# The first three token tiles in one layout, scales in the first transfer, ten products of ones, and two sums moved to GpSimd

## The chip, the cores and the metric

The kernel runs on one core of a Trainium2 chip. The metric is the device time of one execution in microseconds; the kernel is timed in several runs, and the median counts. One further execution is taken with the hardware profiler on. Engine names in profiles: PE is TensorE (matrix products), PEld its weight loads, DVE is VectorE, ACT is ScalarE, POOL is GpSimd, SP is SyncE, which issues most DMA transfers.

## The reference

One encoder layer is applied to two sequences, of 256 and of 2048 tokens, with 1024 features each, in float32:

```python
def encoder_layer(x, w_in, rpb, w_fourier, b_fourier, g_pre, g_na, g_f, w_out, g_post):
    h = rms_norm(x, g_pre)
    proj = h @ w_in
    q, k, v, z_a, u_f, z_f = jnp.split(proj, [...], axis=-1)   # six parts of 512 columns
    y_a = neighbourhood_attention(q, k, v, rpb)     # 8 heads of 64, window of 8 x 16 on a grid 64 wide
    y_f = fourier_mix(u_f, w_fourier, b_fourier)    # real part of a 2-D FFT, then a 512 x 512 product
    mixed = jnp.concatenate([rms_norm(y_a, g_na) * jax.nn.silu(z_a),
                             rms_norm(y_f, g_f) * jax.nn.silu(z_f)], axis=-1)
    out = mixed @ w_out
    return x + rms_norm(out, g_post)
```

## The kernel before

Every float32 product is made of three products: each operand is split into a high half (a cast, by ScalarE) and a low half (what is left over, by VectorE), and `mm3` (lines 159 to 162) adds high x high, high x low and low x high in PSUM. So nearly every operand costs one ScalarE pass and one VectorE pass over an SBUF tile before TensorE can use it. High halves have names ending in `h`, low halves in `l` (`wh`, `wl`; `xh`, `xl`; `vh`, `vl`).

The order of the instructions of every engine around the change is written by hand: each engine runs its own queue in program order and waits on semaphores. Stages in the order of the program, as far as the change touches them:

1. *Products of ones.* `onesq`, a 128 x 128 tile of ones, is set on GpSimd, and TensorE multiplies it with itself 13 times (line 225) while the first data travel.
2. *The start* (lines 611 to 639). The first three token tiles (two of the short sequence, `xt`; one of the long one, `xs`) hold 128 tokens each, with the 1024 features on the partitions in eight chunks of 128. They are loaded in four parts `kp` of two chunks each, one transfer of 128 KB per tile and part (`x_part`): the first part on ScalarE's queue, the others on SyncE's. The weights `wv` come on SyncE's queue, as does `gpre`, the eight chunks of norm scales. `split_w` makes the weights' halves, multiplied by the scales; `x_split` makes those of the tokens. The first useful product needs the first chunk of weights, the scales and the first token tile.
3. *Projections of three more tiles* (line 714 on). When `c == 4`, `xp` is made from the two tiles of the short sequence, the scales, and the tokens' norm factors, which come back from DRAM as a row broadcast over the partitions (`iv_get`, into a tile of the pool tag `vw`).
4. *Sixteen blocks for the short sequence* (lines 756 to 793). Block `b` multiplies one 128-column piece of `w_in` with the 256 tokens: 8 chunks x 3 products of 256 columns, 24 in all. `b_raw(b + 2)` splits the weights for two blocks later (ScalarE line 562 or 565, VectorE line 563 or 566). In between, VectorE prepares operands for the next stage, which forms its products from sums and differences of token quarters `nq` (512 token columns by four chunks, 128 x 2048 per tile): `n_scale` multiplies them by scale and norm factor (blocks 2 to 7), `n_sum` makes four sums (blocks 8 to 11, line 423), `n_first` splits the results (blocks 5, 12, 13; line 428 on ScalarE, line 429 on VectorE). Blocks 14 and 15 split the first weights of the next stage (`op_split`, lines 477 and 478).

The four sums depend on each other: the first writes a tile of its own, `t3`; the second overwrites `(0, 1)`, which the first reads; the third reads `t3` and overwrites `(0, 0)`, which the second reads; the fourth reads what the third wrote. Later in the kernel the same kind of work is done for the other half of the tokens, and there `b_split` (line 439) makes two of the low halves on GpSimd.

Of the kernel before, what the change touches and what calls it, by code (L numbers as in the profile page):

```python
# [10 lines left out]
F32 = mybir.dt.float32  # L11
F32R = mybir.dt.float32r
AF = mybir.ActivationFunctionType
ALU = mybir.AluOpType
# [3 lines left out]
TP, TS = 256, 2048  # L18
T = TP + TS
D = 1024  # L20
KC = 8
# [99 lines left out]
def layout(inp):  # L121
    a = {}
    x = np.concatenate([inp["x_prompt"].reshape(TP, D), inp["x_sample"].reshape(TS, D)], 0)
    a["xn"] = x
    a["xt"] = x[:TP].reshape(4, 2, 32, KC, 128).transpose(1, 4, 3, 0, 2).reshape(2, 128, KC, 128)
    a["xs"] = x[TP:TP + 1024].reshape(4, 4, 2, 32, KC, 128).transpose(0, 2, 5, 4, 1, 3).reshape(8, 128, KC, 128)
    a["xm"] = np.concatenate([x[:TP].reshape(4, 2, 32, D).transpose(1, 0, 2, 3).reshape(2, 128, D),
                              x[TP:].reshape(2, 16, 2, 32, D).transpose(0, 2, 1, 3, 4).reshape(16, 128, D)])
    a["xq"] = x[TP:].reshape(2, 4, 4, 2, 32, 2, 4, 128).transpose(0, 5, 3, 7, 6, 1, 2, 4).reshape(2, 2, 2, 128, 4, 512)
    w = inp["w_in"][0].reshape(KC, 128, 6, 512)  # L130
    q, k, v, za, u, zf = [w[:, :, i] for i in range(6)]
    a["wv"] = v.reshape(2, 4, 128, 512).transpose(0, 2, 1, 3)
    a["wu"] = u.reshape(4, 2, 128, 512).transpose(0, 2, 1, 3)
    a["wz"] = np.stack([m[:, :, h * 128:(h + 1) * 128].transpose(1, 0, 2) for m in (zf, za, k, q) for h in range(4)])
    rpb = inp["rpb"][0]

    d = np.arange(40)[None, :] - np.arange(32)[:, None]
    cols = np.clip(np.stack([d, d - 8]) + 15, 0, 30)
    rows = np.arange(4)[None, :] - np.arange(4)[:, None] + 7
    a["tp"] = rpb[:, rows[:, None, None, :, None], cols[None, :, :, None, :]].reshape(4, 2, 4, 2, 32, 4, 40) \  # L140
        .transpose(0, 2, 4, 3, 1, 5, 6).reshape(4, 128, 640)
    d = np.arange(32)[None, :] - np.arange(16)[:, None]
    cols = np.clip(np.concatenate([d[:, :24], d - 8, d[:, :24] - 8], 1) + 15, 0, 30)
    rows = np.clip(np.arange(15)[None, :] - np.arange(8)[:, None] + 3, 0, 14)
    a["tr"] = rpb[:, rows[:, None, :, None], cols[None, :, None, :]].reshape(8, 128, 1200)
    a["wf"] = inp["w_fourier"][0].reshape(4, 128, 512).transpose(1, 0, 2)
    a["bf"] = inp["b_fourier"][0].reshape(4, 128).T
    a["gpre"] = inp["g_pre"][0].reshape(KC, 128).T
    a["gmix"] = np.concatenate([inp["g_na"][0], inp["g_f"][0]]).reshape(8, 128).T
    a["wo"] = inp["w_out"][0].reshape(2, 4, 128, D)  # L150
    a["gpost"] = inp["g_post"][0].reshape(1, D)
    return {k: np.ascontiguousarray(v) for k, v in a.items()}
# [12 lines left out]
def build(tc, A, O):  # L165
    nc = tc.nc
# [28 lines left out]
    gpre = cst.tile([128, KC], F32, name="gpre")  # L195
# [12 lines left out]
    hp = ph.enter_context(tc.tile_pool(name="hp", bufs=1))  # L208
    st = ph.enter_context(tc.tile_pool(name="st", bufs=2))
# [11 lines left out]
    nc.gpsimd.memset(onesq, 1.0)  # L221

    idle = ps.tile([128, 512], F32, tag="c", name="idle", bufs=1)
    for x in range(13):
        nc.tensor.matmul(idle[:, :128], onesq, onesq, start=True, stop=True)

    def gt(shape, dtype, name):
        return gp.tile(shape, dtype, tag="g", name=name)

    def load(shape, src, name):  # L230
        t = gt(shape, F32, name)
        nc.sync.dma_start(t, src)
        return t

    US = [128, 2, 512]
    BS = [128, KC, 128]
    W = {"v": [], "u": []}
# [12 lines left out]
    def split_w(m, src, ks=range(2)):  # L250
        for k in ks:
            h, l = chunk(), chunk()
            g = gpre[:, len(W[m]):len(W[m]) + 1]
            nc.scalar.activation(h, src[:, k], AF.Copy, scale=g)
            nc.vector.scalar_tensor_tensor(out=l, in0=src[:, k], scalar=g, in1=h.bitcast(F32),
                                           op0=ALU.mult, op1=ALU.subtract)
            W[m].append((h, l))
# [9 lines left out]

    PL = [(None, b) for b in range(2)] + [(s, b) for s in range(NS) for b in range(2)]

    def xsrc(c):  # L270
        return A["xt"][c] if c < 2 else A["xs"][c - 2]

    def row_tile(c):
        s, b = PL[c]
        return c if s is None else 2 + 4 * b + s

    def xload(c):
        xs[c] = load(BS, xsrc(c), "xr")

    def x_split(c, ks=slice(0, 8)):  # L280
        if c not in xh:
            xh[c] = gt(BS, F32R, "xh"), gt(BS, F32R, "xl")
        h, l = xh[c][0][:, ks], xh[c][1][:, ks]
        nc.scalar.copy(h, xs[c][:, ks])
        nc.vector.tensor_tensor(out=l, in0=xs[c][:, ks], in1=h.bitcast(F32), op=ALU.subtract)


    def rows_load(i):
# [19 lines left out]
    ivb, ivr = {}, {}  # L308
# [8 lines left out]
        nc.sync.dma_start(ivD[c0:c0 + n], t)  # L317

    def iv_get(c0, n):
        t = ivb[c0] = hp.tile([128, 1024], F32, tag="vw", name="iv", bufs=3)  # L320
        nc.sync.dma_start(t[:, :128 * n],
                          ivD[c0:c0 + n].rearrange("(o c) p -> o (c p)", o=1).to_broadcast([128, 128 * n]))

# [57 lines left out]
    nq = {}  # L381
# [36 lines left out]
    def n_sum(x):  # L418
        if x == 0:
            nq["t3"] = k8(F32, "nt")  # L420
        o, i0, i1, op = (("t3", (1, 1), (0, 1), ALU.subtract), ((0, 1), (0, 1), (0, 0), ALU.subtract),
                         ((0, 0), "t3", (0, 0), ALU.add), ((1, 0), (0, 0), (1, 0), ALU.subtract))[x]
        nc.vector.tensor_tensor(out=nq[o], in0=nq[i0], in1=nq[i1], op=op)

    def n_first(j):
        src = nq[((0, 0), (1, 0), (0, 0), (0, 1), "t3", (1, 0), (1, 1))[j]]
# [177 lines left out]
    acc, xs, xh, xm = {}, {}, {}, {}  # L604
# [3 lines left out]
    part = lambda a, kp: a[:, kp % 2 * 2:kp % 2 * 2 + 2]  # L608


    def x_part(c, kp):
        if kp == 0:
            xs[c] = gt(BS, F32, "xr")
        ks = slice(2 * kp, 2 * kp + 2)
        (nc.sync if kp else nc.scalar).dma_start(xs[c][:, ks], xsrc(c)[:, ks])

    nc.sync.dma_start(RV[0][:, 0], A["wv"][0][:, 0])
    nc.sync.dma_start(gpre, A["gpre"])
    x_part(0, 0)
    x_part(1, 0)  # L620
    nc.sync.dma_start(RV[0][:, 1], A["wv"][0][:, 1])
    x_part(2, 0)
    nc.scalar.preload_act_table_set("natural_log_exp_and_others")
    nc.scalar.copy(warm, ones)
    for kp in range(4):
        ks = slice(2 * kp, 2 * kp + 2)
        v = part(RV[kp // 2], kp)
        if kp:
            nc.sync.dma_start(v, part(A["wv"][kp // 2], kp))
            for c in range(3):  # L630
                x_part(c, kp)
        split_w("v", v[:, 0:1], (0,))
        x_split(0, ks)
        if kp == 0:
            x_split(1, ks)
        split_w("v", v[:, 1:2], (0,))
        if kp:
            x_split(1, ks)
        x_split(2, ks)
# [74 lines left out]
    for c in range(3, 6):  # L714
        if c == 3:
            iv_get(0, 2)
        if c < 5:
            wz_load(3)
            x_split(c + 1)
        if c == 3:  # L720
            r_put(1)
        if c == 4:
            n_load((0, 0))
            iv_get(2, 8)
            r_put(2)
            xp = k8(F32, "xp", (128, KC, 256))
            hp_, lp_ = [k8(F32R, "p" + x, (128, KC, 256)) for x in "hl"]
            for k in range(KC):
                for t in range(2):
                    ts = slice(128 * t, 128 * t + 128)  # L730
                    nc.vector.scalar_tensor_tensor(out=xp[:, k, ts], in0=xs[t][:, k], scalar=gpre[:, k:k + 1],
                                                   in1=ivb[0][:, ts], op0=ALU.mult, op1=ALU.mult)
            nc.scalar.copy(hp_, xp)
            nc.vector.tensor_tensor(out=lp_, in0=xp, in1=f_(hp_), op=ALU.subtract)
        if c == 5:
            n_load((1, 0))
            b_raw(0)
            b_raw(1)
        p_mm("v", c, range(4))
        vu_out("v", c)  # L740
        if c == 5:
            b_raw(2)
            b_raw(3)
            wz_load(1)
            n_load((0, 1))
            n_scale(None, 0, 0)
            n_first(0)
        p_mm("u", c, range(4))
        if c == 3:
            iv_rows(2, 8)  # L750
        vu_out("u", c)
        if c == 3:
            iv_put(2, 8)


    for b in range(16):
# [13 lines left out]
        if 2 <= b < 8:  # L770
            x, y = divmod(b, 2)
            n_scale(None, *divmod(x, 2)[::-1], range(2 * y, 2 * y + 2))
        elif 8 <= b < 12:
            n_sum(b - 8)
        if b in (5, 12, 13):
            n_first((5, 12, 13).index(b) + 1)
        if b > 13:
# [1 line left out]
        p = mmt(512)[:, :TP]  # L779
# [3 lines left out]
        o = st.tile([128, 256], F32, tag="f", name="f", bufs=3)  # L783
# [51 lines left out]
    for i in range(16):  # L835
# [15 lines left out]
        o = [st.tile([128, 1024], F32, tag="f", name="f", bufs=3) for x in range(2)]  # L851
# [32 lines left out]
        for j in range(7):  # L884
            for f, d in ((u_load, 0), (u_split, 4), (u_stage1, 6)):
                x = 7 * pr + j - 7 - d
# [59 lines left out]
            p = mmt(512)  # L946
# [858 lines left out]
```

## Time and profile before

| | |
|---|---|
| median of 3 runs | 966.51 us (965.75 to 966.55) |
| the profiled execution, its own time | 965.94 us |
| its span, first to last instruction | 964.1 us |
| mean granted TensorE clock | 0.999 |
| TensorE busy | 955.2 us |
| VectorE busy | 703.4 us |
| ScalarE busy | 496.7 us |
| GpSimd busy | 427.0 us |

In the profile's rows, a time in front is the start in microseconds from the first instruction, then the duration; `L423` is a line of the kernel before; `out<-in` names tiles; `x4` is a count, and a row with a count shows the first start and the time that all of them cover. In square brackets stands how long the engine stood idle before the row, and what ended that.

### The profile page before, as it was taken

How to read it: one execution, taken by the hardware profiler on the slowest of the kernel's cores; microseconds unless marked ns; L12 is line 12 of the kernel's file. 1: busy time of each engine (PE TensorE's matmuls, PEld its weight loads, DVE VectorE, ACT ScalarE, POOL GpSimd, SP SyncE). 2: the span in 40 equal slices, each digit the busy share in tenths (PEclk: the TensorE clock that was granted, in tenths of full speed). 3: DMA queues.
4: the chain of work that ended last, by engine and by line, in shares of the span. 5: the costliest groups of instructions: out<-in, count | busy, mean ns of one | idle time of the engine just before them, and what ended most of it. 6: DMA issues, size and time to landing. Idle time of an engine off the chain costs nothing.

```text
span 964.1 us, 16993 instructions
## 1 busy us (share of the span) xinstructions
PE 955.2 (99%) x5743; PEld 799.0 (83%) x5743; DVE 703.4 (73%) x1310; ACT 496.7 (52%) x1077; POOL 427.0 (44%) x400
## 2 busy tenths in 40 slices
PE   9999999999999999999999999999999999999997
PEld 7889988888888888888888889888788887888886
DVE  5768978787876855687877458776765656659997
ACT  5845676423334532233344267677666676644443
POOL 2200002464751202674665043577677686524544
PEclk9999999999999999999999999999999999999999
DMA  8899796557848883499888896598877998979993
GB/s 304 317 354 380 248 348 243 199 203 263 298 185 345 299 347 123 181 362 360 308 294 327 306 335 225 169 285 292 258 235 238 287 285 286 301 253 346 332 353 122
DMA packets 140942, 269.81 MB, mean 280 GB/s; under 512 B 13402, under 2 KB 81840, under 8 KB 137464
## 3 DMA queue, kind: packets, MB, share of 16 engines
q1 hardware_dynamic: 140360, 268.32, 79.8%
q8 instruction: 46, 0.75, 0.3%
q10 hardware_dynamic: 432, 0.39, 0.2%
q14 instruction: 40, 0.33, 0.1%
q0 software_dynamic: 64, 0.02, 0.0%
HBM read 179.00 MB, written 96.81 MB: 286 GB/s over the span
## 4 chain that ended last, share of the span: by engine, by line
PE 96%; DVE 1%; DMA 1%; issue 0%; ACT 0%; DVEq 0%; SPq 0%; ACTq 0%
PE po L1454 20%; PE mm L161 18%; PE mm L160 18%; PE mm L162 18%; PE pv L1543 6%; PE ptb L1527 6%; PE s L1185 4%; PE pab L1022 2%; DMA wr<-wo 1%; PE py L160 1%; DMA gpre<-gpre 0%; PE py L162 0%; PE py L161 0%; PE ppq L1060 0%; PE pz L162 0%
## 5 line engine op out<-in xcount | busy, mean ns | idle before, releaser
L160 PE MATMUL mm<-xh,wa 128*128 128x512 f32 x448 | 174.4, 389 | 0.0
L162 PE MATMUL mm<-xh,wa 128*128 128x512 f32 x448 | 174.3, 389 | 0.0
L161 PE MATMUL mm<-xl,wa 128*128 128x512 f32 x448 | 174.3, 389 | 0.0
L532 POOL TENSOR_TENSOR ws<-wr 128x512 f32<-128x512 f32 x16 | 23.7, 1480 | 221.0 <-DVE vuo L505 123.8
L1219 POOL TENSOR_SCALAR w<-w,m 128x465 f32<-128x465 f32 (+9 forms) x136 | 84.7, 635 | 43.5 <-DVE m L1216 34.0
L162 PEld LDWEIGHTS mm<-xh,wa 128*128 128x128 f32 x448 | 84.1, 188 | 17.6
L160 PEld LDWEIGHTS mm<-xh,wa 128*128 128x128 f32 x448 | 84.1, 188 | 17.6
L161 PEld LDWEIGHTS mm<-xl,wa 128*128 128x128 f32 x448 | 84.1, 188 | 17.4
L1454 PE MATMUL po<-wo,yh 128*128 128x512 f32 x272 | 90.5, 414 | 0.0
L547 DVE TENSOR_TENSOR wa<-wr,wa 128x512 fp32r<-128x512 f32 x60 | 72.8, 1222 | 21.8 <-ACT wa L546 21.3
L1454 PE MATMUL po<-w,yh 128*128 128x512 f32 x280 | 86.8, 391 | 0.0
L1212 ACT ACTIVATE w<-w,m 128x465 f32<-128x465 f32 (+9 forms) x136 | 78.3, 579 | 13.3 <-DVE m L1207 12.9
L1207 DVE CUSTOM_DVE_ANT_1 w<-s,tb 128x465 f32<-128x465 f32 (+8 forms) x124 | 61.2, 531 | 9.8 <-PE s L1185 9.3
L161 PE MATMUL mm<-vl,xh 128*128 128x512 f32 x168 | 65.5, 390 | 0.2 <-DVE vl L478 0.2
L162 PE MATMUL mm<-vh,xl 128*128 128x512 f32 x168 | 65.4, 389 | 0.0
L160 PE MATMUL mm<-vh,xh 128*128 128x512 f32 x168 | 65.4, 389 | 0.0
L585 POOL TENSOR_TENSOR mt<-mt,rmask 128x880 f32<-128x880 f32 (+2 forms) x24 | 50.3, 2110 | 32.2 <-DVE mt L581 25.9
L1454 PEld LDWEIGHTS po<-w,yh 128*128 128x128 f32 x280 | 52.2, 188 | 10.9 <-issue 0.4
L1531 DVE COPY pt<-ptb 120x384 f32<-120x384 f32 (+5 forms) x72 | 40.5, 563 | 27.6 <-PE ptb L1527 27.4
L873 DVE TENSOR_TENSOR f<-u,mm 128x512 f32<-128x512 f32 x64 | 43.5, 679 | 22.3 <-PE mm L162 13.6
L546 ACT CAST wa<-wr 128x512 fp32r<-128x512 f32 x60 | 36.5, 618 | 44.7 <-PE mm L162 18.2
L1527 PE MATMUL ptb<-ident,w 128*120 128x128 f32 (+8 forms) x422 | 58.9, 276 | 0.0
(265 smaller groups left out, 2387.4 us busy)
## 6 DMA issues: line engine op xcount, KB each, us to landing
wr<-wz SPq DMA_DIRECT2D x48, 512.0 KB
vl<-sD SPq DMA_DIRECT2D x20, 512.0 KB
xm<-xm SPq DMA_DIRECT2D x9, 1024.0 KB
oD<-ofs SPq DMA_DIRECT2D x18, 512.0 KB
of<-oD SPq DMA_DIRECT2D x18, 512.0 KB
yr<-yD SPq DMA_DIRECT2D x34, 256.0 KB
zD<-f SPq DMA_DIRECT2D x16, 512.0 KB
xD<-nx SPq DMA_DIRECT2D x14, 512.0 KB
```

Source lines behind the costliest of these rows:

```text
L160: nc.tensor.matmul(out, lh, rh, start=first, stop=False)
L161: nc.tensor.matmul(out, lh, rl, start=False, stop=False)
L162: nc.tensor.matmul(out, ll, rh, start=False, stop=last)
L547: nc.vector.tensor_tensor(out=o[:, 1], in0=src, in1=o[:, 0].bitcast(F32), op=ALU.subtract)
L585: nc.gpsimd.tensor_tensor(out=o, in0=i, in1=rmask[:, m0:m0 + n].unsqueeze(2).to_broadcast([128, n, 80]), op=ALU.add)
L873: nc.vector.tensor_tensor(out=dst(f, b), in0=src(uu[u]), in1=src(p), op=op)
L1207: nc.vector.tensor_tensor_reduce(out=rows(g["w"][b][:, h, :n], w), in0=rows(g["s"][2 * b + h][:, :nr * sw(w)], sw(w))[:, :, :w], in1=tv, s ...
L1212: nc.scalar.activation(w, w, AF.Exp, bias=m[:, h:h + 1], scale=-1.0, accum_out=m[:, 2 + h:3 + h])
L1219: nc.gpsimd.tensor_scalar(w, w, m[:, 4 + h:5 + h], 1.0, ALU.mult, ALU.mult)
L1454: nc.tensor.matmul(p, (d["l"] if x == 2 else d["h"])[:, c], w(n, int(x == 1), c), start=j == 0, stop=j == 11)
L1527: nc.tensor.transpose(ptb[h][:nk, j * 128:j * 128 + 128], g["w"][b][:, h, c0:c0 + nk], ident)
L1543: nc.tensor.matmul(p[hs, b], g["v"][:nk, v, hs], g["pt"][b][:nk, h, j * 128:j * 128 + 128], start=j == 0, stop=j == len(ch) - 1)
```

## The change

- The host lays the first three token tiles side by side: part `kp` of all three is one array of 768 columns. Part 0 carries the norm scales in front of it and goes in two transfers on ScalarE's queue, scales and two tiles first, the third tile second. Parts 1 to 3 are one transfer each on SyncE's queue. `gpre` is no longer loaded; VectorE copies it out of part 0 after the first token split, and the first two weight splits read their scales from part 0 directly.
- Parts 0 and 1 live in tiles of the tag `vw`, parts 2 and 3 in the general pool `g`. As `vw` has three buffers, the two-tile norm row goes to the tag `e`.
- Ten products of ones instead of 13.
- Of the four sums, the first and the fourth are made by GpSimd, the second and third stay on VectorE. They are issued in blocks 8, 10, 11 and 12 instead of 8, 9, 10 and 11.

```diff
+    xt = x[:TP].reshape(4, 2, 32, KC, 128)...        # as before
+    xs = x[TP:TP + 1024].reshape(4, 4, 2, 32, KC, 128)...
+    x0 = np.concatenate([xt, xs[:1]]).reshape(3, 128, 4, 2, 128).transpose(2, 1, 0, 3, 4).reshape(4, 128, 768)
+    a["x0"] = np.concatenate([inp["g_pre"][0].reshape(KC, 128).T, x0[0, :, :512]], 1)
+    a["x2"] = x0[0, :, 512:]
+    a["x1"] = x0[1:]
+    a["xs"] = xs[1:]
-    a["gpre"] = inp["g_pre"][0].reshape(KC, 128).T
...
-    for x in range(13):
+    for x in range(10):
         nc.tensor.matmul(idle[:, :128], onesq, onesq, start=True, stop=True)
...
-            g = gpre[:, len(W[m]):len(W[m]) + 1]
+            x = len(W[m])
+            g = x0[0][:, x:x + 1] if m == "v" and x < 2 else gpre[:, x:x + 1]
...
-        nc.scalar.copy(h, xs[c][:, ks])
-        nc.vector.tensor_tensor(out=l, in0=xs[c][:, ks], in1=h.bitcast(F32), op=ALU.subtract)
+        src = x_first(c, ks.start // 2) if c < 3 else xs[c][:, ks]
+        nc.scalar.copy(h, src)
+        nc.vector.tensor_tensor(out=l, in0=src, in1=h.bitcast(F32), op=ALU.subtract)
...
-        t = ivb[c0] = hp.tile([128, 1024], F32, tag="vw", name="iv", bufs=3)
+        t = ivb[c0] = st.tile([128, 512], F32, tag="e", name="iv", bufs=6) if n == 2 else \
+            hp.tile([128, 1024], F32, tag="vw", name="iv", bufs=3)
...
-        nc.vector.tensor_tensor(out=nq[o], in0=nq[i0], in1=nq[i1], op=op)
+        (nc.vector if x in (1, 2) else nc.gpsimd).tensor_tensor(out=nq[o], in0=nq[i0], in1=nq[i1], op=op)
...
-    def x_part(c, kp):
-        if kp == 0:
-            xs[c] = gt(BS, F32, "xr")
-        ks = slice(2 * kp, 2 * kp + 2)
-        (nc.sync if kp else nc.scalar).dma_start(xs[c][:, ks], xsrc(c)[:, ks])
+    x0 = [hp.tile([128, 776], F32, tag="vw", name="x0", bufs=3)]
+    x0.append(hp.tile([128, 768], F32, tag="vw", name="x0", bufs=3))
+    x0.extend(gt([128, 768], F32, "x0") for kp in range(2))
+
+    def x_first(c, kp):
+        return x0[kp][:, 8 * (kp == 0):][:, :768].rearrange("p (c k t) -> p c k t", c=3, t=128)[:, c]
 
     nc.sync.dma_start(RV[0][:, 0], A["wv"][0][:, 0])
-    nc.sync.dma_start(gpre, A["gpre"])
-    x_part(0, 0)
-    x_part(1, 0)
+    nc.scalar.dma_start(x0[0][:, :520], A["x0"])
+    nc.scalar.dma_start(x0[0][:, 520:], A["x2"])
     nc.sync.dma_start(RV[0][:, 1], A["wv"][0][:, 1])
-    x_part(2, 0)
...
             nc.sync.dma_start(v, part(A["wv"][kp // 2], kp))
-            for c in range(3):
-                x_part(c, kp)
+            nc.sync.dma_start(x0[kp], A["x1"][kp - 1])
         split_w("v", v[:, 0:1], (0,))
         x_split(0, ks)
         if kp == 0:
+            nc.vector.tensor_copy(gpre, x0[0][:, :8])
             x_split(1, ks)
...
-        elif 8 <= b < 12:
-            n_sum(b - 8)
+        if b in (8, 10, 11, 12):
+            n_sum((8, 10, 11, 12).index(b))
```

In line 731 the source of `xp` becomes `x_first(t, k // 2)[:, k % 2]`, the same columns in the new layout.

More of the change, by code (lines that the diff above doesn't have):

```diff
@@ L124, in layout @@
     a["xn"] = x
-    a["xt"] = x[:TP].reshape(4, 2, 32, KC, 128).transpose(1, 4, 3, 0, 2).reshape(2, 128, KC, 128)
-    a["xs"] = x[TP:TP + 1024].reshape(4, 4, 2, 32, KC, 128).transpose(0, 2, 5, 4, 1, 3).reshape(8, 128, KC, 128)
+    xt = x[:TP].reshape(4, 2, 32, KC, 128).transpose(1, 4, 3, 0, 2).reshape(2, 128, KC, 128)
+    xs = x[TP:TP + 1024].reshape(4, 4, 2, 32, KC, 128).transpose(0, 2, 5, 4, 1, 3).reshape(8, 128, KC, 128)
+    x0 = np.concatenate([xt, xs[:1]]).reshape(3, 128, 4, 2, 128).transpose(2, 1, 0, 3, 4).reshape(4, 128, 768)
[3 more added lines that the diff above has]
+    a["xs"] = xs[1:]
     a["xm"] = np.concatenate([x[:TP].reshape(4, 2, 32, D).transpose(1, 0, 2, 3).reshape(2, 128, D),
@@ L268, in build @@
     PL = [(None, b) for b in range(2)] + [(s, b) for s in range(NS) for b in range(2)]
-    def xsrc(c):
-        return A["xt"][c] if c < 2 else A["xs"][c - 2]
     def row_tile(c):
@@ L277, in xload @@
     def xload(c):
-        xs[c] = load(BS, xsrc(c), "xr")
+        xs[c] = load(BS, A["xs"][c - 3], "xr")
     def x_split(c, ks=slice(0, 8)):
@@ L730, in build @@
                     ts = slice(128 * t, 128 * t + 128)
-                    nc.vector.scalar_tensor_tensor(out=xp[:, k, ts], in0=xs[t][:, k], scalar=gpre[:, k:k + 1],
+                    nc.vector.scalar_tensor_tensor(out=xp[:, k, ts], in0=x_first(t, k // 2)[:, k % 2], scalar=gpre[:, k:k + 1],
                                                    in1=ivb[0][:, ts], op0=ALU.mult, op1=ALU.mult)
```

## The prediction

> **What bounds the kernel now.** I read the page first: busy shares, then the chain that ended last.
>
> ```profile
> span 964.1 us, 16993 instructions
> ...
> PE 955.2 (99%) x5743; PEld 799.0 (83%) x5743; DVE 703.4 (73%) x1310; ACT 496.7 (52%) x1077; POOL 427.0 (44%) x400
> ...
> PE 96%; DVE 1%; DMA 1%; issue 0%; ACT 0%; DVEq 0%; SPq 0%; ACTq 0%
> ```
>
> TensorE (PE) is busy for 99% of the span and carries 96% of the chain. Nothing in the change takes a useful product away, so it can only move the moment the first useful product starts, or open and close gaps between products. The view of PE's waits lists all the gaps there are.
>
> ```profile
> PE mm L160 <- ACT xh L284: 0.5, 1, 0.5
> PE py L160 <- DVE Y L1294: 0.2, 1, 0.2
> PE mm L161 <- DVE vl L478: 0.2, 1, 0.2
> ```
>
> The first lies before the first useful product. The last is where the two moved sums were meant to help, at 119.9 us. More than a few tenths cannot be won there. What can be lost there is a matter of VectorE (DVE), whose timeline just before shows no idle time at all. Columns are start, duration, engine, line, operation.
>
> ```profile
> 98.64 1.22 DVE L563 TENSOR_TENSOR wl<-wr,wh 128x1024 fp32r<-128x1024 f32 x1
> 99.78 2.28 DVE L423 TENSOR_TENSOR nt<-nx 128x2048 f32<-128x2048 f32 x1
> 101.98 1.22 DVE L563 TENSOR_TENSOR wl<-wr,wh 128x1024 fp32r<-128x1024 f32 x1
> 103.11 2.28 DVE L423 TENSOR_TENSOR nx<-nx 128x2048 f32<-128x2048 f32 x1
> 105.32 1.22 DVE L566 SCALAR_TENSOR_TENSOR wl<-wr,wh 128x1024 fp32r<-128x1024 f32 x1
> ...
> 109.79 2.28 DVE L423 TENSOR_TENSOR nx<-nx 128x2048 f32<-128x2048 f32 x1
> ...
> 113.13 2.28 DVE L429 TENSOR_TENSOR xl<-nx,xh 128x2048 fp32r<-128x2048 f32 x1
> 115.33 1.22 DVE L566 SCALAR_TENSOR_TENSOR wl<-wr,wh 128x1024 fp32r<-128x1024 f32 x1
> 116.47 2.28 DVE L429 TENSOR_TENSOR xl<-nx,xh 128x2048 fp32r<-128x2048 f32 x1
> 118.67 4.62 DVE L478 TENSOR_TENSOR vl<-vr,vh 128x1024 fp32r<-128x1024 f32 x4
> ```
>
> Each `wl` is the low half of one block's weights (`b_raw`, two blocks ahead), each L423 a sum of token operands (`n_sum`). A `wl` and a sum take 3.3 us start to start; PE needs one `wl` per block of 24 products. The pace of PE, from a window over six blocks and from its timeline:
>
> ```profile
> 98.97:116.24 17.27, 17.27 (x146) 17.27 (x145) 17.27 (x11) 12.30 (x15) 0.00 (x0) 1.00 0.81 281
> 116.61 0.39 PE L162 MATMUL mm<-ph,wl 128*128 128x256 f32 x1
> 119.94 0.50 PE L161 MATMUL mm<-vl,xh 128*128 128x512 f32 x1 [0.21 <-DVE vl L478]
> ```
>
> 144 products (146 less two that reach in) in 17.27 us are 0.12 us each, 2.88 us a block. Against 3.3 us DVE loses its lead, and by block 15 it has none: `wl` of 115.33 ends at 116.55, and the third product, the first that needs it, starts at 116.61. Any DVE delay from here on is a PE delay.
>
> **The change, the two sums.** The edit puts the first and the last of the four sums on GpSimd (POOL), idle at that time, and moves the second and third one block later. POOL does such a pass in this kernel, at 309 us (`b_split`), beside DVE:
>
> ```profile
> 309.02 5.47 POOL L439 TENSOR_TENSOR xl<-xl,xh 128x2048 fp32r<-128x2048 f32 x1 [28.28 <-ACT xh L438]
> 318.26 5.14 POOL L439 TENSOR_TENSOR xl<-xl,xh 128x2048 fp32r<-128x2048 f32 x1 [3.77 <-ACT xh L438]
> 307.65 2.35 DVE L478 TENSOR_TENSOR vl<-vr,vh 128x1024 fp32r<-128x1024 f32 x2
> 310.52 6.19 DVE L478 TENSOR_TENSOR vl<-vr,vh 128x1024 fp32r<-128x1024 f32 x2
> 316.63 2.28 DVE L439 TENSOR_TENSOR xl<-xl,xh 128x2048 fp32r<-128x2048 f32 x1
> 318.84 0.68 DVE L873 TENSOR_TENSOR f<-u,mm 128x512 f32<-128x512 f32 x1
> 321.93 3.62 DVE L439 TENSOR_TENSOR xl<-xl,xh 128x2048 fp32r<-128x2048 f32 x1 [2.42 <-ACT xh L438]
> ```
>
> The same pair of DVE instructions takes 2.35 us at 307.65 and 6.19 us at 310.52, inside POOL's. It ends at 316.71, 2.2 us after POOL's end at 314.49: DVE stood still until POOL was done. At 321.93 again, ending 2.15 us after POOL's end at 323.40. In the other direction, POOL ends 4.49 us after the DVE work that ran when it was issued (314.49 less 310.00; 323.40 less 318.91). The instruction at 318.84, which reads a product in `mm`, isn't held up. So two-input passes over SBUF tiles on these two engines exclude each other, one whole instruction at a time, and a 2048-wide one holds DVE for 4.5 us less an overlap of 0.13 us. Every DVE row from 98.64 to 118.67 is of that kind. A sum that costs DVE 2.2 us at home costs it 4.4 us on POOL, unless DVE would have idled.
>
> Now the chain, in the times of before:
> - Sum 1 can start when the last scaled operand is ready, at 98.7; `wl` of 98.64 has started already, so POOL goes from 99.86 to 104.35. Queued behind on DVE is `wl` of block 11, whose `wh` is there long before; it ends at 105.44 instead of 103.20. PE wants it for the third product of block 11, at 116.49 - 4 x 2.88 = 104.97. PE waits 0.5 us.
> - DVE then does `wl`, sum 2, `wl`, sum 3, `wl` without a break, at 1.13 and 2.2 us each: 105.35 to 113.25, sum 3 done at 112.1. Blocks 12 to 14 get their weights in time.
> - The next DVE instruction (L429) needs a copy that ScalarE makes of sum 3:
>
> ```profile
> 109.09 1.90 ACT L428 CAST xh<-nx 128x2048 fp32r<-128x2048 f32 x1
> ```
>
> - It is ready at 114.0. POOL's sum 4 has waited only for sum 3 and for DVE's `wl`, so it starts first: 113.25 to 117.74. L429 goes from 117.6 to 119.9, and behind it in DVE's queue stands `wl` of block 15, done at 121.0.
> - PE wants that at 116.49 + 0.5 = 117.0 and gets it at 121.1: 4.1 us.
> - Block 15 ends at 123.7; the next L429 and the first `vl` end at 124.4, where PE waits some 0.4 us, in place of 119.94.
>
> PE is at 124.4 where it was at 119.94: 4.5 us late, and as it is busy all the way to its last product it can't catch up. The work that comes after is moved with PE and keeps its room. Bounds for POOL's pass: 4.5 us by both rows above, 5.3 us by twice the mean of POOL's 1024-wide differences, which include waits for DVE. With 5.3 the sum is 6.1 us; I take 4.5, the same width.
>
> ```profile
> L408 POOL TENSOR_TENSOR nx<-nx 128x1024 f32<-128x1024 f32 x8 | 21.2, 2651 | 1.3 <-DMA xD<-nx 0.8
> ```
>
> **The change, the start.** The chain view and the timelines of the first microseconds:
>
> ```profile
> 1.17 4.62 DMA gpre<-gpre
> 5.88 0.72 ACT wc L254
> 0.99 5.48 PE L225 MATMUL idle<-onesq 128*128 128x128 f32 x26 [0.99 <-POOL onesq L221]
> 6.95 0.50 PE L160 MATMUL mm<-wc,xh 128*128 128x512 f32 x1 [0.49 <-ACT xh L284]
> 2.58 3.38 SPq L615 DMA_DIRECT2D xr<-xt  x2
> SPq L615 <- DMA xr<-xt: 2.6, 1, 2.6
> ```
>
> The scales (4 KB) land at 5.79 and let ScalarE make the first weights; 1.16 us later PE starts. The change puts them in front of two tiles' parts, in one 260 KB transfer on ScalarE's queue. The last two rows say when the old first transfer there, half as large, landed: SyncE issues an x part at 2.58 (an issue takes 0.4 us) and then stands 2.6 us until the first of the x transfers has landed, at 5.6. So the new one can hardly land before 5.6, only 0.2 us sooner than the scales did; with 128 KB more in it, at the 237 GB/s moved early on or the 406 GB/s of a full stretch, 0.3 to 0.5 us later.
>
> ```profile
> 2.00:3.00 1.00, 1.00 (x6) 1.00 (x6) 0.00 (x0) 0.87 (x1) 0.00 (x0) 1.00 1.01 237
> 6.00:7.00 1.00, 0.51 (x6) 0.32 (x4) 0.36 (x1) 1.00 (x3) 0.00 (x0) 1.00 1.02 406
> ```
>
> Ends: -0.2 to +0.4 us. I take 0, since one landing replaces the later of two. Three products of ones fewer cost nothing by themselves: PE's start waits for data. Ten end at 0.99 + 20 x 0.21 = 5.2 us, with PE idle until 6.9. SyncE issues three x transfers for nine and one load of scales fewer, so its 2.6 us wait goes and later loads come earlier; PE waits for none of them in before, so that wins nothing. The DVE copy of the scales (128x8), the other pool for the two-tile `iv` and the new view in L731 are tenths of a microsecond beside PE's products, and hidden: PE's list of waits has no gap between the first useful product and 119.9 us.
>
> **Sum.** 4.5 us on the profiled execution of 965.9 us (span 964.1 us and 1.8 us around it) is 970.4 us. The median of the three runs is 0.6 us above that execution: 971.0 us. This forecast has a chance of 0.62 and a range of its own of 970.8 to 973.0 (start and POOL's pass at their bounds).
>
> **Rivals.**
> *Faster or level: POOL doesn't hold DVE up here.* Then DVE saves 4.4 us, the two small PE delays go (116.61 for 116.49, 119.94 for 119.58, together 0.4 us), and the start may gain from -0.4 to, at the very most, the 1.7 us to the end of the ten products of ones. That is 964.4 to 966.5 us. For it speaks that POOL has nothing else to do there and that ScalarE, not DVE, could be what a DVE row waits for; against it, the two rows at 310.52 and 321.93. It decides if DVE runs its `wl` rows in 1.2 us while POOL is busy. The Trainium skill, in "Perfetto Trace Analysis", section "Optimizing Scalar/DVE Operations", says that moving work from a saturated VectorE even to GpSimd may make sense, and words the exclusive lock for DVE's two-port modes only, while warning that the move might not help; by its first half the time would be this rival's, by the rows above it is not. Chance 0.14.
>
> *Only the first sum hurts.* If sum 4 fits between DVE's instructions, L429 runs at 114.0, block 15's `wl` ends at 117.4, and the first `vl` at 120.8: 0.9 us late, 967.4 us. It would need POOL to pause; no row shows that. Chance 0.08.
>
> *The clock.* The products of ones also bring PE to full pace:
>
> ```profile
> 1.36:5.62 4.26, 4.26 (x21) 4.26 (x21) 1.00 0.76 198
> 5.85:6.30 0.45, 0.45 (x5) 0.42 (x4) 1.00 1.08 426
> 957.20:961.80 4.60, 0.00 (x0) 0.98 0.44 166
> 961.80:964.10 2.30, 0.00 (x0) 0.50 0.34 127
> ```
>
> They stand 0.2 us apart until 5.6 and 0.1 us after 5.85; at the end the clock falls to 0.50 some 4.4 us after the last product. With ten, PE rests from 5.2 to 6.9 just when the full pace came, and later for 4.1 us. If either leaves PE at half pace for some 3 us, that is 1.5 us more: 972.5 us. The skill's "TensorE: Matmul & The Clock Gate", section "Part 1: The HAM clock gate", has the clock set by free-running windows of 3.4 us; by it the 4.1 us rest can hold one whole window and halve the clock. Chance 0.16.
>
> **The numbers.** A measurement of this kernel tells about 0.2% (1.9 us) from no change. Faster by more is the far end of the first rival, 0.06; within it, its rest and most of the second, 0.14; slower, 0.80. The range of 967.0 to 973.2 us holds the forecast, the clock and most of the second rival, some 0.82.
>
> **What would show it.** In the changed profile: two POOL rows of 128x2048 near 99 and 113 us; the `wl` of block 11 lasting over 4 us and L429 behind sum 4 likewise; new PE waits of 0.5 and 4 us for `wl`; the first useful product between 6.7 and 7.4 us. I am wrong if DVE's rows beside POOL's keep 1.2 and 2.3 us, or if PE shows no wait near 117 us.

## Result

| | before | changed |
|---|---|---|
| median of 6 runs | 966.24 us (965.75 to 966.55) | 971.32 us (970.07 to 971.77) |
| profiled execution, own time | 965.9 us | 971.37 us |
| its span | 964.1 us | 969.6 us |

The ratio of the times is 1.005, with a 95% interval of 1.0037 to 1.0063. In the profile page of the changed kernel TensorE's busy time is up by only 1.6 us (955.2 before), and the chain holds more VectorE work than before (2% for 1%):

```profile
span 969.6 us, 16970 instructions
...
PE 956.8 (99%) x5737; PEld 801.0 (83%) x5737; DVE 712.0 (73%) x1309; ACT 497.3 (51%) x1077; POOL 440.7 (45%) x402
...
PE 95%; DVE 2%; issue 1%; DMA 1%; ACT 1%; DVEq 0%; ACTq 0%
```

The view of PE's waits has two rows that were not there before. (In the changed kernel the lines of `wl` are L567 and L570, of `n_sum` L427, of `n_first` L432 and L433, of `vl` L482, of `mm3` L164 to L166.)

```profile
PE mm L166 <- DVE wl L570: 3.8, 1, 3.8
...
PE mm L164 <- ACT xh L287: 0.4, 1, 0.4
PE mm L166 <- DVE wl L567: 0.4, 1, 0.4
```

One wait of 3.8 us for the weight of block 15 and one of 0.4 us for that of block 11. The DVE timeline of the changed kernel shows why they are late:

```profile
97.78 1.22 DVE L567 TENSOR_TENSOR wl<-wr,wh 128x1024 fp32r<-128x1024 f32 x1
99.70 4.86 DVE L567 TENSOR_TENSOR wl<-wr,wh 128x1024 fp32r<-128x1024 f32 x1 [0.71 <-ACT wh L566]
...
111.16 1.21 DVE L570 SCALAR_TENSOR_TENSOR wl<-wr,wh 128x1024 fp32r<-128x1024 f32 x1
113.22 5.80 DVE L433 TENSOR_TENSOR xl<-nx,xh 128x2048 fp32r<-128x2048 f32 x1 [0.84 <-ACT xh L432]
118.94 1.21 DVE L570 SCALAR_TENSOR_TENSOR wl<-wr,wh 128x1024 fp32r<-128x1024 f32 x1
...
122.28 4.62 DVE L482 TENSOR_TENSOR vl<-vr,vh 128x1024 fp32r<-128x1024 f32 x4
```

and its POOL timeline which instructions they stood behind:

```profile
98.08 5.41 POOL L427 TENSOR_TENSOR nt<-nx 128x2048 f32<-128x2048 f32 x1 [70.61 <-DVE nx L404]
111.37 5.50 POOL L427 TENSOR_TENSOR nx<-nx 128x2048 f32<-128x2048 f32 x1 [7.89 <-DVE nx L427]
```

A `wl` of 1.22 us takes 4.86, an L433 of 2.28 us takes 5.80. Each time POOL was issued while a DVE row ran (97.78 to 99.00, 111.16 to 112.37). Its own row counts the wait for that row's end and ends 4.49 and 4.50 us after it, at 103.49 and 116.87. The DVE row that was issued meanwhile ends 1.1 and 2.15 us after POOL: its own length, less a short overlap. The two engines take turns, by whole instructions.

What PE makes of it, from its timeline; columns are start, duration, and in brackets the idle time before:

```profile
120.21 0.58 PE L166 MATMUL mm<-ph,wl 128*128 128x256 f32 x1 [3.81 <-DVE wl L570]
120.59 0.41 PE L164 MATMUL mm<-ph,wh 128*128 128x256 f32 x1
120.80 0.41 PE L165 MATMUL mm<-pl,wh 128*128 128x256 f32 x1
...
125.50 0.63 PE L165 MATMUL mm<-vl,xh 128*128 128x512 f32 x1
```

Block 15's product of `wl` starts at 120.21 instead of 116.61, 3.6 us late. The first product with `vl` starts at 125.50 instead of 119.94, which is 5.56 us late, and without any wait. The 2 us between were lost while PE was busy: after the wait the products stand 0.21 us apart instead of 0.12. In the window view of the changed kernel (columns: window, length, busy time of PE, PEld, DVE, ACT, POOL, then the granted TensorE clock, DMA share, GB/s):

```profile
116.12:119.53 3.41, 0.27 (x3) 0.07 (x1) 3.41 (x2) 3.41 (x7) 0.75 (x1) 1.00 0.12 41
119.53:122.94 3.41, 2.73 (x13) 2.73 (x14) 3.41 (x3) 0.99 (x2) 0.00 (x0) 0.50 0.11 36
122.94:126.36 3.42, 3.42 (x15) 3.13 (x15) 3.42 (x4) 1.00 (x2) 0.00 (x0) 0.50 0.00 0
```

PE was busy for 0.27 of 3.41 us during the wait, and from 119.53 to 126.36 us the clock was granted at half. That is twice 3.41 us, and the two long stretches at full clock in this trace, of 112.64 and 839.68 us, are 33 and 246 times that. The Trainium skill, in "TensorE: Matmul & The Clock Gate", section "Part 1: The HAM clock gate", has the clock set by free-running windows of 3.41 us; with that the trace agrees.

The start went the other way. The chain of the changed kernel in its first microseconds:

```profile
0.73 4.18 DMA x<-x
...
4.93 0.72 ACT wc L259
5.65 0.30 ACT xh L287
...
6.00 0.79 PE mm L164
```

The first useful product starts at 6.00 instead of 6.95: the transfer with the scales lands at 4.91, where the scales by themselves landed at 5.79. (That is one profile of each kernel; a second one with the old layout, below, has the scales at 5.12.) So the profiled execution sums to 0.95 us less at the start, two waits of 4.2 us together in place of one of 0.2, and some 2 us at half clock; that is about 5.1, and the span is 5.5 us longer. Some 0.3 us more lie in the first products with `vl`, which ran at half clock too: the fifth product of that stage, at 126.60 us and again at full clock, is 5.84 us behind its place in the kernel before (120.76), where the second, the first with `vl`, was 5.56 behind.

### The profile page after: what moved, and what is told of

Its sections match the earlier page's. It is cut to its first block, busy times and chain, and to the rows that moved or that the text cites. A ratio compares the mean times of both kernels' runs of the same rounds, so it can differ in the third digit from the quotient of the medians.

```text
span 969.6 us, 16970 instructions
## 1 busy us (share of the span) xinstructions
PE 956.8 (99%) x5737; PEld 801.0 (83%) x5737; DVE 712.0 (73%) x1309; ACT 497.3 (51%) x1077; POOL 440.7 (45%) x402
## 4 chain that ended last, share of the span: by engine, by line
PE 95%; DVE 2%; issue 1%; DMA 1%; ACT 1%; DVEq 0%; ACTq 0%
PE po L1457 20%; PE mm L164 18%; PE mm L166 18%; PE mm L165 18%; PE pv L1546 6%; PE ptb L1530 6%; PE s L1188 4%; PE pab L1025 2%; DMA wr<-wo 1%; PE py L164 1%; PE py L166 0%; PE py L165 0%; DVE nx L427 0%; DMA x<-x 0%; PE ppq L1063 0%
## 5 line engine op out<-in xcount | busy, mean ns | idle before, releaser
L164 PE MATMUL mm<-xh,wa 128*128 128x512 f32 x448 | 174.4, 389 | 0.0
L166 PE MATMUL mm<-xh,wa 128*128 128x512 f32 x448 | 174.3, 389 | 0.0
L164 PEld LDWEIGHTS mm<-xh,wa 128*128 128x128 f32 x448 | 84.1, 188 | 17.7
L166 PEld LDWEIGHTS mm<-xh,wa 128*128 128x128 f32 x448 | 84.1, 188 | 17.4
L164 PE MATMUL mm<-vh,xh 128*128 128x512 f32 x168 | 65.6, 391 | 0.0
L166 PE MATMUL mm<-vh,xl 128*128 128x512 f32 x168 | 65.6, 390 | 0.0
```

The source lines that it names most:

```text
L164: nc.tensor.matmul(out, lh, rh, start=first, stop=False)
L166: nc.tensor.matmul(out, ll, rh, start=False, stop=last)
```

## The experiments

Theory: two sums on POOL hold VectorE and thereby PE (some 4 us), and the wait itself halves PE's clock (some 1.5 us); the start wins a few tenths. Rivals: the layout's moved transfers cost time; the wait is the whole loss; only one of the sums does harm; POOL's sums could be made harmless by cutting them. Unless an edit shows otherwise, it is made in the changed kernel. The kernel before was run beside each; it gave 965.89 us beside the first four, 966.21 beside the next four, 966.12 and 966.29 beside the others. I compare by the difference to these.

**All sums back on VectorE** (the layout and ten products of ones stay).

```diff
-        (nc.vector if x in (1, 2) else nc.gpsimd).tensor_tensor(out=nq[o], in0=nq[i0], in1=nq[i1], op=op)
+        nc.vector.tensor_tensor(out=nq[o], in0=nq[i0], in1=nq[i1], op=op)
...
-        if b in (8, 10, 11, 12):
-            n_sum((8, 10, 11, 12).index(b))
+        elif 8 <= b < 12:
+            n_sum(b - 8)
```

> The changed kernel with all four sums back on VectorE in blocks 8 to 11; the new layout and the ten products of ones stay. If the two sums on GpSimd are the whole loss (the theory of the record), what is left is the earlier start, 0.95 us in the profile: first useful product near 6.0 us, no PE wait over 0.3 us after it, clock at full from about 7 us, 965.1 us. Rival: the new layout or the ten products cost something of their own, later or in other executions: 966.2 us or more.

Measured: 965.66 us, 0.23 under the kernel before and between the two times expected; ratio 0.9993 (0.9982 to 1.0003). The whole loss is gone, and the wait for `vl` is the one of before:

```profile
PE mm L165 <- DVE vl L482: 0.2, 1, 0.2
```

The layout and the shorter row of ones cost nothing; what they win can't be told from nothing. The first useful product starts at 6.12 us here.

**The two sums alone**, in the kernel before, old layout and 13 products of ones.

```diff
-        nc.vector.tensor_tensor(out=nq[o], in0=nq[i0], in1=nq[i1], op=op)
+        (nc.vector if x in (1, 2) else nc.gpsimd).tensor_tensor(out=nq[o], in0=nq[i0], in1=nq[i1], op=op)
...
-        elif 8 <= b < 12:
-            n_sum(b - 8)
+        if b in (8, 10, 11, 12):
+            n_sum((8, 10, 11, 12).index(b))
```

> The kernel before with only the two sums on GpSimd and the four sums in blocks 8, 10, 11 and 12; old layout, 13 products of ones. Theory of the record: the two PE waits of 0.5 and 4 us appear near 105 and 117 us and nothing else changes, 970.7 us; with the clock halved after the long wait, as in the profile of the changed kernel, 972.5 us. Rival, that the loss belongs to the new layout: 966.2 us, no PE wait over 0.3 us.

Measured: 972.23 us, 6.3 over the kernel before; ratio 1.007 (1.0056 to 1.0084). Its PE waits are those of the changed kernel:

```profile
PE mm L162 <- DVE wl L566: 3.8, 1, 3.8
...
PE mm L162 <- DVE wl L563: 0.4, 1, 0.4
```

Here, too, the clock falls behind the wait, for 3.41 us instead of 6.83:

```profile
116.64:120.05 3.41, 0.00 (x0) 0.00 (x0) 3.41 (x2) 3.41 (x6) 0.44 (x1) 1.00 0.21 72
120.05:123.46 3.41, 3.04 (x14) 3.04 (x15) 3.41 (x3) 0.68 (x1) 0.00 (x0) 0.50 0.02 5
```

The sums carry all of the loss, and with the old transfers it is no smaller. One thing more is in this profile: its transfers are those of the kernel before, and yet the scales land at 5.12 and the first useful product starts at 6.28 us, not at 5.79 and 6.95. So the start moves by 0.67 us from one profile of the same transfers to another.

**The sums cut in four.** GpSimd makes each of its two sums in four instructions of 128x512, so that VectorE can come in between.

```diff
-        (nc.vector if x in (1, 2) else nc.gpsimd).tensor_tensor(out=nq[o], in0=nq[i0], in1=nq[i1], op=op)
+        if x in (1, 2):
+            nc.vector.tensor_tensor(out=nq[o], in0=nq[i0], in1=nq[i1], op=op)
+        else:
+            for k in range(4):
+                nc.gpsimd.tensor_tensor(out=nq[o][:, k], in0=nq[i0][:, k], in1=nq[i1][:, k], op=op)
```

> The changed kernel, each of the two GpSimd sums as four instructions of 512 columns instead of one of 2048. If GpSimd and VectorE exclude each other one whole instruction at a time, VectorE now waits at most 1.3 us per instruction and the two take turns: weights of block 15 come about 2 us sooner, the long PE wait falls from 3.8 to about 1.7 us, the clock stays at full, about 967.3 us. Rival, that GpSimd's pass slows VectorE in proportion to its bytes or time, however it is cut: the wait stays near 3.8 us and the time at 971.3 us or above.

Measured: 970.17 us, 4.3 over the kernel before; ratio 1.0042 (1.003 to 1.0055). The changed kernel was 5.1 us over; a gain near 4 us was expected, and the 0.8 us between the two are within their intervals: a miss. Its timelines on POOL and on VectorE, and its PE waits:

```profile
111.00 10.98 POOL L431 TENSOR_TENSOR nx<-nx 128x512 f32<-128x512 f32 x4 [7.89 <-issue]
```

```profile
112.85 2.47 DVE L437 TENSOR_TENSOR xl<-nx,xh 128x2048 fp32r<-128x2048 f32 x1 [0.84 <-ACT xh L436]
115.24 2.32 DVE L574 SCALAR_TENSOR_TENSOR wl<-wr,wh 128x1024 fp32r<-128x1024 f32 x1
117.48 3.38 DVE L437 TENSOR_TENSOR xl<-nx,xh 128x2048 fp32r<-128x2048 f32 x1
120.78 5.69 DVE L486 TENSOR_TENSOR vl<-vr,vh 128x1024 fp32r<-128x1024 f32 x4
```

```profile
PE mm L165 <- DVE vl L486: 2.4, 1, 2.4
...
PE mm L166 <- DVE wl L574: 0.9, 1, 0.9
PE mm L166 <- DVE wl L571: 0.8, 1, 0.8
```

VectorE does come in between, and pays a piece of about 1.1 us at each of its next instructions (2.32 for 1.21, 3.38 for 2.28, 5.69 for 4.62). The waits still sum to 4.1 us. Cutting spreads the loss and leaves its sum as it was, since VectorE has no slack. Spread out, the waits leave the clock alone in this profile: none of the three stretches of 3.41 us in which they fall has less than 2.11 us of products.

```profile
115.22:118.63 3.41, 2.47 (x21) 2.27 (x20) 3.41 (x3) 3.41 (x6) 3.41 (x2) 1.00 0.11 38
118.63:122.04 3.41, 2.11 (x17) 1.79 (x15) 3.41 (x2) 2.97 (x4) 3.35 (x2) 1.00 0.17 58
122.04:125.46 3.42, 2.34 (x10) 1.97 (x11) 3.42 (x4) 0.73 (x1) 0.00 (x0) 1.00 0.84 236
```

(These stretches are counted back in steps of 3.41 us from 961.72, where the clock falls at the end of this profile.)

**The wait filled.** Fourteen more calls of products of ones (28 instructions) stand before block 15, where PE waits anyway.

```diff
+        if b == 15:
+            fill = ps.tile([128, 512], F32, tag="c", name="fill", bufs=1)
+            for x in range(14):
+                nc.tensor.matmul(fill[:, :128], onesq, onesq, start=True, stop=True)
```

> The changed kernel with 14 more products of ones (3 us) in PE's queue just ahead of block 15, inside the long wait; nothing waits for them. If the rest of 3.8 us lets the clock fall to half, and the products of block 15 and the next few at half pace cost 2 us, this keeps the clock at full and gives about 969.3 us with the wait for the weights ending at the same time. Rival, that the clock costs nothing (PE only waits for VectorE anyway): 971.3 us.

Measured: 969.93 us, 4.0 over the kernel before; ratio 1.0041 (1.0029 to 1.0054). There are more instructions on the busiest engine, and the time is no longer than the changed kernel's, 5.1 us over. PE's timeline:

```profile
117.75 3.29 PE L786 MATMUL fill<-onesq 128*128 128x128 f32 x28
...
121.96 0.38 PE L166 MATMUL mm<-ph,wl 128*128 128x256 f32 x1 [0.69 <-DVE wl L570]
122.18 0.28 PE L164 MATMUL mm<-ph,wh 128*128 128x256 f32 x1
122.30 0.28 PE L165 MATMUL mm<-pl,wh 128*128 128x256 f32 x1
```

The wait now ends at 121.96, and behind it the products stand 0.12 us apart at once. From the first product of `wl` to the first with `vl` they take 3.34 us here, 4.31 in the profile of the two sums alone (half clock for 3.41 us) and 5.29 in that of the changed kernel (for 6.83 us). So in the profiles the lost clock costs 1 or 2 us. In the medians it is 1 us (5.1 less 4.0), but the intervals of the two ratios overlap: the size is not shown by the medians alone. The wait by itself costs some 4 us.

The 121.96 can't be compared with the 120.21 of the changed kernel, because this whole profile is 1.7 us late from its start: its first products stand 0.43 us apart until 10.6 us, against 0.23 in the kernel with all sums at home.

```profile
8.02 0.63 PE L165 MATMUL mm<-wc,xh 128*128 128x512 f32 x1
8.45 0.63 PE L166 MATMUL mm<-wc,xl 128*128 128x512 f32 x1
```

**Only the first sum on GpSimd** (the other three on VectorE in blocks 10, 11 and 12).

```diff
-        (nc.vector if x in (1, 2) else nc.gpsimd).tensor_tensor(out=nq[o], in0=nq[i0], in1=nq[i1], op=op)
+        (nc.vector if x else nc.gpsimd).tensor_tensor(out=nq[o], in0=nq[i0], in1=nq[i1], op=op)
```

> The changed kernel with only the first sum on GpSimd; sums two to four on VectorE in blocks 10, 11 and 12. By whole-instruction exclusion the first sum costs VectorE 3.6 us at the weights of block 11 and its absence gives 2.2 us back: PE waits 0.4 us near 104 us and, as VectorE no longer catches up, 1.5 to 2.5 us in all up to the first low half of the next stage; no wait over 3 us, so the clock stays at full after it: 967.5 us. The rival of the record, that GpSimd does not hold VectorE or that the first sum is harmless: 965.7 us, as with all sums at home.

Measured: 967.20 us, 1.0 over the kernel before and 1.2 over the kernel with all sums at home; ratio to before 1.0007 (0.9998 to 1.0016). Its waits:

```profile
PE mm L166 <- DVE wl L570: 1.6, 1, 1.6
...
PE mm L166 <- DVE wl L567: 0.4, 1, 0.4
```

The first sum has its price even when VectorE keeps the last one: the delay of block 11 is carried on to block 15. The waits show it; the median alone doesn't, since its interval holds 1.

**Only the last sum on GpSimd** (sums 1 to 3 on VectorE in blocks 8, 10 and 11).

```diff
-        (nc.vector if x in (1, 2) else nc.gpsimd).tensor_tensor(out=nq[o], in0=nq[i0], in1=nq[i1], op=op)
+        (nc.gpsimd if x == 3 else nc.vector).tensor_tensor(out=nq[o], in0=nq[i0], in1=nq[i1], op=op)
```

> The changed kernel with sums 1 to 3 on VectorE (in blocks 8, 10 and 11) and only the last sum, in block 12, on GpSimd. If the two engines exclude each other for whole instructions: the weight of block 11 is undisturbed, the sum that starts the next stage is held to some 5.8 us at 110 to 113, the weight of block 15 is about 2 us late, and TensorE waits about 2.2 us there and 0.5 us at the first value product; no wait passes 3.4 us, so the clock stays full, and the median is about 968.1 us (2.4 above the kernel with all sums on VectorE). First alone (+1.5) and last alone (+2.4) then come to less than both (+5.6), the rest being the halved clock. Rival, the last sum carries the whole loss, clock included: 971 us. Rival, it carries nothing: 965.7 us.

Measured: 968.34 us (967.15 to 971.54), 2.2 over the kernel before and 2.45 over all sums at home; ratio to before 1.0022 (1.0013 to 1.0031). First and last alone come to 1.2 + 2.45 = 3.7 us over all sums at home, both together to 5.3; the filled wait came to 4.3. What goes beyond the parts, 1.6 us, is about what the clock can cost, but that split isn't shown, for the last sum alone can lose clock as well. One thing expected was wrong: I took the clock for safe where no wait passes 3.4 us. Its profiled execution has a wait of 2.5 us and half the clock behind it, as its waits and windows show:

```profile
PE mm L166 <- DVE wl L570: 2.5, 1, 2.5
```

```profile
116.23:119.64 3.41, 1.27 (x11) 1.07 (x9) 3.41 (x2) 3.41 (x6) 0.43 (x1) 1.00 0.21 71
119.64:123.05 3.41, 3.05 (x14) 3.05 (x15) 3.41 (x3) 0.70 (x1) 0.00 (x0) 0.50 0.02 6
```

This execution was the longest of the eleven, 971.54 us against 967.15 to 969.56 for the others. Its products also ran at half pace at the start, until 10.4 us, which cost some 1.6 us more. That fits a clock which falls in some executions of one kernel and not in others, but the others have no profile, so it is not shown.

What the falls in these profiles go with is not the length of the wait, but how much of one such stretch of 3.41 us it takes. With the stretches counted from the clock's own changes, the clock of the thirteen profiles, from 8 us on, fell behind each that held 2.10 us of products or less (0.00, 0.27 and 1.27 in the three falls at these blocks, the others at the end of the kernel) and behind none that held 2.11 or more. It came back behind half-clock stretches of 3.04, 3.05 and 3.41 us of products and not behind the one of 2.73, after which the changed kernel had a second.

**A copy in place of the last sum.** The same kernel, but GpSimd copies one operand of the last sum and leaves out the subtraction: one tile read instead of two.

```diff
-        (nc.gpsimd if x == 3 else nc.vector).tensor_tensor(out=nq[o], in0=nq[i0], in1=nq[i1], op=op)
+        if x == 3:
+            nc.gpsimd.tensor_copy(nq[o], nq[i0])
+        else:
+            nc.vector.tensor_tensor(out=nq[o], in0=nq[i0], in1=nq[i1], op=op)
```

> As the kernel with only the last sum on GpSimd, but GpSimd copies one operand there instead of subtracting two (the fourth sum's subtraction is left out): one input in place of two, at the same place and of the same 128x2048 size. If a GpSimd pass holds VectorE only where it reads two tiles: VectorE's L437-type pass behind it keeps 2.3 us in place of 5.8, TensorE has no wait for the weight of block 15, and the median is 965.5 to 966. Rival, any GpSimd pass over SBUF of this width holds VectorE: a held VectorE row again, a wait for the weight of block 15, and 967 to 968.3 us by the copy's length.

Measured: 964.67 us, 1.6 under the kernel before; ratio 0.9991 (0.9982 to 1.0). The time is a little under the first theory's, and there is no wait for the weight of block 15; but the held row is the rival's, as POOL and VectorE show:

```profile
109.38 2.76 POOL L428 COPY nx<-nx 128x2048 f32<-128x2048 f32 x1 [81.96 <-DVE nx L430]
```

```profile
109.17 1.22 DVE L573 SCALAR_TENSOR_TENSOR wl<-wr,wh 128x1024 fp32r<-128x1024 f32 x1
111.23 3.06 DVE L436 TENSOR_TENSOR xl<-nx,xh 128x2048 fp32r<-128x2048 f32 x1 [0.85 <-ACT xh L435]
```

POOL ends at 112.14, 1.75 us after the `wl` of 109.17; L436 ends at 114.29, again 2.15 us after POOL. The copy holds VectorE too, only for 1.75 us instead of 4.5, half of which VectorE would have idled for ScalarE's copy. The price goes by how long POOL takes, and not by its reading two tiles.

**The scales by themselves.** All sums on VectorE; the scales are a transfer of their own on SyncE's queue again, the tokens keep the new layout.

```diff
-            g = x0[0][:, x:x + 1] if m == "v" and x < 2 else gpre[:, x:x + 1]
+            g = gpre[:, x:x + 1]
...
-    nc.scalar.dma_start(x0[0][:, :520], A["x0"])
+    nc.sync.dma_start(gpre, A["gpre"])
+    nc.scalar.dma_start(x0[0][:, 8:520], A["x0"])
```

> All sums on VectorE, new layout, ten products of ones, but the scales again in a transfer of their own on SyncE's queue behind the first weights, as before. If the late scales were what held the first product, it starts near 6.9 us again, 966.2 us. Rival, that what starts it earlier is the new layout (rows of 2 KB in place of 1 KB, fewer transfers in flight), and the scales land with the weights: first product near 6.0 us, 965.7 us.

Measured: 966.23 us, level with the kernel before; ratio 1.0000 (0.9991 to 1.0008). Its chain starts with the scales, and PE starts at 6.36, between the 6.9 and the 6.0 that were expected:

```profile
1.17 4.04 DMA gpre<-gpre
...
5.29 0.72 ACT wc L260
...
6.36 0.80 PE mm L165
```

**Thirteen products of ones**, all sums on VectorE, new layout.

```diff
-    for x in range(10):
+    for x in range(13):
```

> All sums on VectorE, new layout, 13 products of ones instead of 10. If ten products often leave PE at half pace for its first useful products (full clock came at 6.9 and at 10.6 us in two profiles with ten, 5.6 and 6.0 us in two others), 13 bring it to full by 6.5 us every time: first useful product 6.3 to 6.6 us, and a median 0.3 us under that of the same kernel with ten, 965.4 us, with a narrower spread. Rival, that the clock does not matter there: the start is 0.3 us later and so is the end, 966.0 us.

Measured: 965.70 us, 0.5 under the kernel before; ratio 0.9992 (0.9983 to 1.0001). With ten it was 0.23 under: the number of ones makes no difference that these medians can tell. The first useful product starts at 5.85 us, sooner than the 6.3 to 6.6 expected. What was asked about the clock shows only in profiles: the half pace at the start is in three of the nine with ten ones (the wait filled, the last sum only, the scales by themselves) and in none of the four with thirteen, and cost 1.2 to 1.7 us each time. Three of nine against none of four can be chance.

**The last sum taken out of the blocks.** All sums on VectorE; the fourth, which the next stage needs only later, is issued there.

```diff
-        elif 8 <= b < 12:
+        elif 8 <= b < 11:
             n_sum(b - 8)
...
+    at(1, n_sum, 3)
```

> All sums on VectorE, new layout, ten products of ones; the fourth sum is taken out of block 11 and made in the next stage, where VectorE had an idle stretch of 1.6 us at 125.5 us. VectorE then has 2.2 us in hand at block 15: the PE waits of 0.2 us at 119.9 us and of 0.1 us at the weights of block 15 go, 965.3 us against 965.7 us with the sum at home. Rival, that the sum then delays the low halves of the next stage: a PE wait near 127 to 140 us and 966 us or more.

Measured: 965.53 us, 0.7 under the kernel before; ratio 0.9991 (0.9983 to 1.0). The wait for `vl` is gone from its list, which was 0.2 us in all: VectorE's load before block 15 is cheaper to delay than to move to another engine.

**Both**: the last sum later, thirteen products of ones; these two edits on top of all sums on VectorE.

```diff
-    for x in range(10):
+    for x in range(13):
...
+    at(1, n_sum, 3)
```

> All sums on VectorE, the last one taken out of block 11 and put into the next stage, the new layout of the first transfers, 13 products of ones. If the small gains at the start and at the first value product both hold: about 965.3 us, under the kernel before (966.2) by 0.1%. Rival, nothing more than the layout's own share: 965.5 to 965.7 us, which can't be told from it.

Measured: 964.51 us (963.70 to 969.45); ratio 0.9992 (0.998 to 1.0004). The median is 1.6 us under that of the kernel before, the interval holds 1: not shown to be faster. Its profile doesn't say why it should be. The wait at the first `vl` is gone, but a later split of the same stage, on another line, now comes late:

```profile
146.72 0.50 PE L165 MATMUL mm<-vl,xh 128*128 128x512 f32 x1 [0.66 <-DVE vl L478]
```

## Why the prediction was right, point by point

**The two engines exclude each other: right.** POOL's rows end 4.49 and 4.50 us after the DVE rows that they waited for; the prediction had 4.49 from 310 and 321 us. VectorE's rows were to end 2.2 us behind POOL's and end 2.15 behind. Its wording was too narrow, since a copy, which reads one tile, held VectorE as well.

**Its way to PE: right in place and order.** Forecast were waits of 0.5 us at block 11 and 4.1 at block 15, with L429 (now L433) first behind POOL and `wl` behind that; the profile has 0.4 and 3.8. A third wait of 0.4 us at the first `vl` did not come, because by then PE was itself later than VectorE: half its clock was gone.

**The clock: a rival that happened beside the forecast, mis-sized.** The forecast's sum had nothing for it; the rival had 1.5 us. The profiles show 1 us for 3.41 us at half clock and 2 us for the 6.83 of the changed kernel; the medians, less surely, 1 us. The rival's first half, half pace at the start, hardly touched the changed profile: the ten products of ones ended at 5.62 us, not at 5.2, the useful ones began at 6.00, not at 6.9, and only the first two were slow. It did come in three other profiles with ten ones, at 1.2 to 1.7 us, and doesn't show in the medians (965.66 us with ten, 965.70 with thirteen).

**The start: the term that failed.** It was put at 0, between -0.2 and +0.4 us, and the changed profile shows -0.95. The step at fault is that the new transfer could hardly land before 5.6, because the old one had not. It landed at 4.91. A queue's old landing time, read from where SyncE went on, was not a bound for another transfer in its place. Nor was one profile a bound for the old start: with the old transfers it was 6.95 in the kernel before and 6.28 with the two sums alone. In the eight profiles with the scales in the tokens' transfer and ten ones, the first useful product starts between 5.84 and 6.13 us, and with the scales by themselves, in either layout, at 6.28, 6.36 and 6.95: that the scales no longer travel by themselves is part of it. Why the tokens' transfer came sooner than the old ones was not settled. Nor does it show in the medians: 0.23 us under the kernel before is within the noise.

**The sum.** 971.0 us was forecast and 971.32 measured, 4.5 and 5.1 us over the kernel before. That they came so near is partly luck, because in the profile two errors met: a start better by nearly 1 us, and a clock worse by 2.

**The rivals.** That POOL doesn't hold VectorE fell with the first held row. What the Trainium skill says first in "Perfetto Trace Analysis", section "Optimizing Scalar/DVE Operations", that moving work even to GpSimd may make sense, is not borne out here; its warning that the move might not help agrees with the 5.1 us lost. The Trainium skill's page "SBUF — State Buffer", section "Who interferes with whom", speaks of an exclusive lock on the port pair which VectorE and GpSimd share, held for a whole instruction, and has VectorE instructions with two SBUF inputs contend with GpSimd ones that read SBUF: the rows at 99.70 and 113.22 agree with that, and so does the row at 111.23 beside the copy. That only the first sum hurts is wrong as well: alone it costs 1.2 us, the last one alone 2.45.

## What to carry to other kernels

An idle engine is no free engine: before work moves from VectorE to GpSimd, look in the same trace for a row of that width beside VectorE rows, and add GpSimd's duration, not VectorE's saving, to VectorE's queue. Where VectorE has no slack, cutting the moved work into pieces spread that price and left the sum of the waits as it was (4.1 us for 4.2); moving it to a later place on its own engine cost nothing. And a gap of a few microseconds on TensorE can cost more than its length, since the clock may fall behind it: price the gap and the slow stretch after it. Before a start is priced by one profile, look for a second one of the same transfers.

## What was not expected of the hardware

A wait of 2.5 us was followed by 3.4 us at half clock in one profile, while waits of 0.8, 0.9 and 2.4 us in another left the clock alone: the first left 1.27 us of products in its stretch of 3.41 us, the others never less than 2.11. A 128x2048 GpSimd copy, worth 1.75 us behind VectorE, held VectorE as surely as the 4.5 us sum did.
